# One block sum moved to VectorE, one gate/up set in plain form, and block sums over both depth halves at once, in a float32 decoder trunk

## The chip, the cores and the metric

The kernel runs on one core of a Trainium2 chip. The metric is the device time of one execution in microseconds (us). A row of times below comes from the hardware profile of one execution.

## What is computed

Four layers run one after the other on 256 tokens of width 1024, all in float32. Each layer is a SwiGLU feed-forward block (FFN), a token mixer with memory attention, and a second FFN, so there are eight FFNs. Only the FFN matters here:

```python
def swiglu_ffn(x, w_gate_up, w_down):
    gate, up = jnp.split(x @ w_gate_up, 2, axis=-1)
    return (jax.nn.silu(gate) * up) @ w_down
x = x + 0.5 * rms_norm(swiglu_ffn(rms_norm(x, g[0]), ffn_w_gate_up[i, 0], ffn_w_down[i, 0]), g[1])
```

The width of `gate` and of `up` is 2816.

## The kernel before, in words

**Precision.** A float32 operand is split in two (L311-313): ScalarE writes a high part `hi`, VectorE subtracts it to get the low part `lo`. A product takes three matmuls: hi·hi, hi·lo, lo·hi. Every weight tile of 128x1024 (512 KB) so costs one `hi` on ScalarE and one `lo` on VectorE before TensorE can use it. Ten such hi/lo pairs exist (the ring); plain weight tiles come through five `raw` buffers, loaded by SyncE in the order of use.

**Sets.** The 2816 columns of gate and up are worked in six sets of 4, 4, 2, 4, 4 and 4 column tiles of 128. Sets 0 and 4 are plain: 4 tiles of gate and 4 of up, each used for both halves of the tokens, 96 matmuls of 128x512 in all. Set 2, the narrow one, has 4 mixed tiles. Between the parts of the sets, `fill` puts in one or two tiles of the down projection (L696, 12 matmuls each).

**The 7-product form.** Sets 1, 3 and 5 (`SEVEN`) treat [two token halves x two depth halves] times [two depth halves x (gate, up)] as a 2x2 block product with 7 block products instead of 8: 84 matmuls of 128x512 (L624) rather than 96. The weight blocks, each a tile `quad` of 128x2x1024 (two quarters of the depth, index h), are x11 (gate, first depth half), x12 (up, first half), x21 (gate, second half) and x22 (up, second half, the far block). The products 0 to 6 use, in order, x11, x21, then x11+x12+x22, x12+x22, then x11+x12, the sum of all four, and x22. These are formed in place, one h at a time:

- x12 += x22, by an accumulating transfer that GpSimd issues (L271, called at L267) as soon as the second operand has been loaded. I call it the first sum.
- x11 += x12, by VectorE (L285), before the split for product 2: the second sum.
- x21 += x11, again by an accumulating transfer (L271, called from L286): the third sum.
- x11 -= x22, by VectorE (L288), before the split for product 4: the difference. It must follow the third sum, which reads x11.

**Joining the products.** `seven` (L636-671) gathers products 0 and 2 and then 3 and 5 in one PSUM bank, 1 in a second, 4 and 6 in a third. A `snap` (L632) on ScalarE copies a bank out before the next product adds to it: the copies after products 0, 2 and 3 are needed by products 2, 3 and 5. After product 4, VectorE computes the closing step of that bank (L655, `c22`: snap = c - U3); product 6 adds to the same bank, so its first matmul waits until the closing step has read it.

**Order.** Python emits the instructions in program order and a scheduler of the framework weaves them; each engine then runs its own list strictly in order. `slot` (called after each weight tile has been used) releases a hi/lo pair, issues one of the eight `quad` loads of the next 7-product set, if any is left, and lets up to two more splits go. The loads of a set are issued from slots of the set before it, on SyncE's queue between the `raw` loads, in the order x11, x21, x12, x22, two halves each; `quads_for` says how many of them a split needs.

Of the kernel before, what the change touches and what calls it, by code (L numbers as in the profile page):

```python
# [15 lines left out]
ALU = mybir.AluOpType  # L16
# [39 lines left out]
WIDTH = (4, 4, 2, 4, 4, 4)  # L56
SETS = len(WIDTH)
FIRST = tuple(sum(WIDTH[:s]) for s in range(SETS))
SEVEN = (1, 3, 5)
FILL = {1: (2, 2), 2: (2,), 3: (2, 0), 4: (1, 1), 5: (2, 2)}  # L60
QUADS = 8


def ffn_chunks(l, f):
    order = []
    nd = 0

    def fill(n):
        nonlocal nd, order
        order += [("D", l, f, nd + i) for i in range(n)]  # L70
        nd += n

    for s in range(SETS):
        if s in SEVEN:
            for ops, n in zip(((0, 1, 2), (3, 4, 5, 6)), FILL[s]):
                order += [("S", l, f, s, op, h) for op in ops for h in range(2)]
                fill(n)
            continue
        for c, n in zip(("e",) if WIDTH[s] == 2 else ("g", "u"), FILL.get(s, (0, 0))):
            order += [(c, l, f, s, i) for i in range(4)]  # L80
            fill(n)
    return order + [("D", l, f, j) for j in range(nd, NF)]
# [23 lines left out]
def plan():  # L106
    order = []
    for l in range(DEPTH):
        kind = l % 3
        order += ffn_chunks(l, 0)  # L110
        cols = [("C", l, c) for c in range(len(MIX_COLS[kind]))]
        for g, rng in enumerate(MIX_GROUPS[kind]):
            if g == 2:
                order += mem_units(l)
            order += [("R", l, g, k, n) for k, n in group_units(group_width(rng))]
            if g == 2:
                order += cols
        if len(MIX_GROUPS[kind]) == 2:
            order += mem_units(l) + cols
        order += [("O", l, j) for j in range(N_OUT[kind])]  # L120
        order += ffn_chunks(l, 1)
    return order
# [83 lines left out]
class Trunk:  # L206
# [53 lines left out]
    def load_quad(self):  # L260
        key = self.quad_loads.popleft()
        q, h = key[4:]
        if h == 0:
            pool, tag = ((self.main, "mgh"), (self.quad_pool, "q22"), (self.main, "mgl"), (self.main, "rows"))[q]
            self.quad[q] = pool.tile([P, 2, 1024], F32, tag=tag, name="quad")
        self.fetch(self.quad[q][:, h, :], key)
        if q == 3:  # L267
            self.gather(self.quad[1][:, h, :], self.quad[3][:, h, :])

    def gather(self, x, y):  # L270
        self.nc.gpsimd.dma_start(out=x, in_=y, accum_op=ALU.add)  # L271
# [1 line left out]
    def quads_for(self, key):  # L273
        if self.quad is None or self.quad_set != key[1:4]:
            return None
        return max(0, len(self.quad_loads) - (QUADS - ((2 * key[4] if key[4] < 2 else 6) + key[5] + 1)))

    def can_split(self):
        key = self.plan[self.split_n]
# [1 line left out]

    def operand(self, op, h):
        b11, b12, b21, b22 = (t if t is None else t[:, h, :] for t in self.quad)
        if op == 2:
            self.nc.vector.tensor_tensor(out=b11, in0=b11, in1=b12, op=ALU.add)  # L285
            self.gather(b21, b11)  # L286
        elif op == 4:
            self.nc.vector.tensor_tensor(out=b11, in0=b11, in1=b22, op=ALU.subtract)  # L288
        return (b11, b21, b11, b12, b11, b21, b22)[op]

    def split_next(self):
# [245 lines left out]
    def ffn(self, l, f, post_next, pre_next, last=False):  # L537
        nc, tc = self.nc, self.tc
        with tc.tile_pool(name=f"ffn{l}{f}", bufs=1, reuse_waits="tile") as fp:
# [8 lines left out]
            def tile_T():  # L548
                return fp.tile([P, 512], F32, tag="T", name="T", bufs=4)
# [21 lines left out]
            def first_set():  # L571
                T[0] = [tile_T(), tile_T()]
                held = [self.take("g", l, f, 0, i) for i in range(4)]
                for t in range(2):
                    g = self.rot()
                    for i in range(4):
                        pair(held[i], g, i, t)
                        self.slot(t)
                    silu(T[0][t], g)
                    u = self.rot()  # L580
                    if t == 0:
                        held.extend(self.take("u", l, f, 0, i) for i in range(4))
                    for i in range(4):
                        pair(held[4 + i], u, i, t)
                        self.slot(t)
                        if t == 0 and i == 2:
                            self.trans(1, keep=self.keep)
                    nc.vector.tensor_tensor(out=T[0][t], in0=T[0][t], in1=u, op=ALU.mult)
# [46 lines left out]
            def seven(s):  # L635
                tt = nc.vector.tensor_tensor  # L636
                v = {}
                a, b = self.rot(), self.rot()
                T0, T1 = T[s]
                keep = lambda n: lambda: v.__setitem__(n, snap(a))  # L640
                product(s, 0, a, True, keep("P1"))

                def c11():
                    tt(out=v["P1"], in0=v["P1"], in1=b, op=ALU.add)
                    silu(T0, v["P1"])

                product(s, 1, b, True, c11)
                turned(s - 1)
                product(s, 2, a, False, keep("U2"))
                fill(FILL[s][0])  # L650
                product(s, 3, a, False, keep("U3"))
                c = self.rot()

                def c22():
                    tt(out=v["U3"], in0=c, in1=v["U3"], op=ALU.subtract)  # L655

                product(s, 4, c, True, c22)

                def c21():
                    silu(T1, a)  # L660
                    tt(out=T1, in0=T1, in1=v["U3"], op=ALU.mult)

                product(s, 5, a, False, c21)

                def c12():
                    tt(out=v["U2"], in0=c, in1=v["U2"], op=ALU.subtract)
                    tt(out=T0, in0=T0, in1=v["U2"], op=ALU.mult)

                product(s, 6, c, False, c12)
                fill(FILL[s][1])  # L670

            self.new_quad(fp, l, f, 1)
            first_set()
            left = sums()
            gn = {"pre": None}
# [37 lines left out]
            for s in range(1, SETS):  # L713
                T[s] = [tile_T(), tile_T()]
                if s + 1 in SEVEN:
                    self.new_quad(fp, l, f, s + 1)
                if s in SEVEN:
                    seven(s)
                    if s == max(SEVEN):
                        self.bg.append(gains)  # L720
                    if s == max(SEVEN) and (l, f) == (0, 0):
                        self.bg.extend(self.setup2())
                    if s == min(SEVEN) and (l, f) == (0, 1):
                        self.bg.extend(self.rope_tables(fp))
# [623 lines left out]
```

## Time and profile before

| | |
|---|---|
| median of 3 runs | 1888.37 us (1885.9 to 1891.17) |
| the profiled execution, its own time | 1888.2 us |
| its span, first to last instruction | 1886.4 us |
| TensorE / VectorE / ScalarE / GpSimd busy | 1842.0 / 1537.1 / 1132.7 / 150.2 us |
| mean granted TensorE clock | 0.996 |
| weight loads of 512 KB through `raw` / `quad` | 440 / 192 |
| accumulating transfers of 512 KB | 96 |

How to read the rows: a row of a timeline gives the start, the length, the engine (PE TensorE, DVE VectorE, ACT ScalarE, POOL GpSimd, SP SyncE; "q" marks its DMA-issuing side), the line of the kernel, the operation, the tile written and the tiles read, the shape and a count; in square brackets stands how long the engine stood idle just before it, and what ended that. A row of the view of waits has who waited, for whom, the total in us, how many times, and the longest. A row of the windows has the stretch, its length, the busy time of PE, PE's weight loads, DVE, ACT and POOL with counts, the granted clock, the DMA share and GB/s.

### The profile page before, as it was taken

What the parts mean: (1) busy time and instruction counts of PE and PEld (TensorE: products, weight loads), DVE (VectorE), ACT (ScalarE), POOL (GpSimd) and SP (SyncE); (2) the same over time, 40 slices, a digit from 0 to 9 for tenths busy, and PEclk for the clock granted to TensorE, in tenths of its full rate; (3) what the DMA queues carried; (4) which work ended last, traced back from release to release, by engine and by line L of the source; (5) the groups of instructions that cost most, each with busy time, mean ns of one, the idle gap of its engine ahead of it and who ended that gap; (6) DMA issues with size and microseconds to landing.
All of it is one profiled execution on the core that took longest, in us unless ns stands there. A gap on an engine that the chain in (4) does not pass through costs nothing.

```text
span 1886.4 us, 25346 instructions
## 1 busy us (share of the span) xinstructions
PE 1842.0 (98%) x9310; PEld 1535.2 (81%) x9310; DVE 1537.1 (81%) x1868; ACT 1132.7 (60%) x1541; POOL 150.2 (8%) x211
## 2 busy tenths in 40 slices
PE   7999999999999999999999999999999999999998
PEld 5788887878788797778878889877788888987886
DVE  6888878987988768888789876879887988879884
ACT  5666656656665655656666666556665666656652
POOL 0000201000100100100010000010001000201000
PEclk9999999999999999999999999999999999999999
DMA  8886748776786662677668667358775786738862
GB/s 295 257 265 225 224 136 264 227 243 223 226 261 194 235 220 101 201 242 247 215 210 263 211 218 257 105 190 256 247 245 169 245 264 204 247 125 273 256 192 78
DMA packets 117692, 413.01 MB, mean 219 GB/s; under 512 B 13620, under 2 KB 18112, under 8 KB 117440
## 3 DMA queue, kind: packets, MB, share of 16 engines
q1 hardware_dynamic: 103568, 359.47, 54.2%
q0 software_dynamic: 14000, 51.92, 13.8%
q8 instruction: 73, 1.20, 0.3%
q14 instruction: 51, 0.42, 0.1%
HBM read 359.95 MB, written 1.06 MB: 191 GB/s over the span
## 4 chain that ended last, share of the span: by engine, by line
PE 41%; DVE 7%; DMA 3%; issue 2%; ACT 1%; POOL 1%; DVEq 0%; ACTq 0%; POOLq 0%
PE acc L696 12%; PE rot L624 9%; PE rot L337 5%; PE rot L339 5%; PE rot L338 5%; DVE lo L313 5%; PE acc L960 2%; DMA quad<-quad 2%; DMA quad<-in_w 1%; PE rot L565 1%; PE acc L880 1%; DVE quad L288 1%; PE rot L894 1%; PE rot L862 1%; ACT hi L312 0%
## 5 line engine op out<-in xcount | busy, mean ns | idle before, releaser
L313 DVE TENSOR_TENSOR lo<-raw,hi 128x1024 fp32r<-128x1024 f32 (+2 forms) x451 | 536.3, 1217 | 77.6 <-ACT hi L312 74.7
L312 ACT ACTIVATE hi<-raw 128x1024 fp32r<-128x1024 f32 (+2 forms) x451 | 463.2, 1051 | 198.3 <-DMA raw<-in_w 96.7
L312 ACT ACTIVATE hi<-quad 128x1024 fp32r<-128x1024 f32 x336 | 343.6, 1053 | 227.5 <-DVE quad L285 131.8
L313 DVE TENSOR_TENSOR lo<-quad,hi 128x1024 fp32r<-128x1024 f32 x336 | 397.5, 1219 | 20.7 <-ACT hi L312 19.9
L339 PE MATMUL rot<-hi,xtl 128*128 128x512 f32 (+3 forms) x816 | 312.8, 384 | 3.9 <-DVE xtl L313 3.9
L337 PE MATMUL rot<-hi,xth 128*128 128x512 f32 (+3 forms) x816 | 315.0, 386 | 0.4 <-ACT hi L312 0.4
L338 PE MATMUL rot<-lo,xth 128*128 128x512 f32 (+3 forms) x816 | 312.0, 382 | 0.3 <-DVE lo L313 0.3
L624 PE MATMUL rot<-hi,sums 128*128 128x512 f32 x768 | 255.1, 398 | 16.2 <-ACT snap L632 8.0
L696 PE MATMUL acc<-hi,hh 128*128 128x512 f32 x640 | 199.4, 391 | 0.0
L696 PE MATMUL acc<-lo,hh 128*128 128x512 f32 x640 | 198.9, 390 | 0.0
L696 PE MATMUL acc<-hi,hl 128*128 128x512 f32 x640 | 197.9, 390 | 0.0
L624 PEld LDWEIGHTS rot<-hi,sums 128*128 128x128 f32 x768 | 145.8, 190 | 52.9 <-ACT snap L632 12.3
L339 PEld LDWEIGHTS rot<-hi,xtl 128*128 128x128 f32 x816 | 153.7, 188 | 37.0 <-DVE xtl L313 8.3
L337 PEld LDWEIGHTS rot<-hi,xth 128*128 128x128 f32 x816 | 153.8, 189 | 29.2 <-ACT hi L312 1.0
L338 PEld LDWEIGHTS rot<-lo,xth 128*128 128x128 f32 x816 | 153.8, 188 | 29.2 <-DVE lo L313 0.5
L624 PE MATMUL rot<-lo,sums 128*128 128x512 f32 x384 | 151.2, 394 | 2.1 <-DVE lo L313 2.1
L271 POOL DMA_DIRECT2D quad<-quad x96 | 83.7, 897 | 837.6 <-DMA quad<-in_w 394.5
L696 PEld LDWEIGHTS acc<-hi,hl 128*128 128x128 f32 x640 | 119.6, 188 | 26.9 <-DVE hl L313 2.2
L696 PEld LDWEIGHTS acc<-lo,hh 128*128 128x128 f32 x640 | 119.9, 188 | 24.7
L696 PEld LDWEIGHTS acc<-hi,hh 128*128 128x128 f32 x640 | 119.7, 188 | 24.5
L624 PE MATMUL rot<-hi,xtl 128*128 128x512 f32 x288 | 112.1, 389 | 0.0
L624 PE MATMUL rot<-hi,xth 128*128 128x512 f32 x288 | 112.0, 389 | 0.0
(214 smaller groups left out, 2571.3 us busy)
## 6 DMA issues: line engine op xcount, KB each, us to landing
raw<-in_w SPq DMA_DIRECT2D x440, 512.0 KB, 4.8
quad<-in_w SPq DMA_DIRECT2D x192, 512.0 KB, 5.1
quad<-quad POOLq DMA_DIRECT2D x96, 512.0 KB, 4.7
gpre<-in_norm_g SPq DMA_DIRECT2D x8, 512.0 KB, 6.3
gpost<-in_norm_g SPq DMA_DIRECT2D x8, 512.0 KB, 3.4
memraw<-in_mem_t SPq DMA_DIRECT2D x32, 128.0 KB, 3.6
g<-in_norm_g SPq DMA_DIRECT2D x8, 512.0 KB, 6.7
raw<-in_w SPq DMA_DIRECT2D x8, 384.0 KB, 4.1
```

What stands on the lines that cost most here:

```text
L271: self.nc.gpsimd.dma_start(out=x, in_=y, accum_op=ALU.add)
L288: self.nc.vector.tensor_tensor(out=b11, in0=b11, in1=b22, op=ALU.subtract)
L312: self.nc.scalar.activation(out=hi, in_=src, func=AF.Copy)
L313: self.nc.vector.tensor_tensor(out=lo, in0=src, in1=hi.bitcast(F32), op=ALU.subtract)
L337: mm(out, a[0], b[0], start=start, stop=False)
L338: mm(out, a[0], b[1], start=False, stop=False)
L339: mm(out, a[1], b[0], start=False, stop=stop)
L565: nc.tensor.transpose(ps[:, k * P:(k + 1) * P], T[s][t][:, k * P:(k + 1) * P], self.ident)
L624: nc.tensor.matmul(ps, a[i], w[j][:, kk, :], start=fresh and h == kk == i == j == 0, stop=h == kk == i == 1, skip_group_check=True)
L696: mm(ys[t][:, n * 512:(n + 1) * 512], x, y[:, 0, n * 512:(n + 1) * 512], start=(j == 0 and x is a[0] and y is w[0]), stop=(j == NF - 1 and ...
L862: nc.tensor.transpose(ps[:, i * P:(i + 1) * P], blocks[b0 + i], self.ident)
L960: self.nc.tensor.matmul(o["y"][t][:, h * 512:(h + 1) * 512], x, y[:, 0, h * 512:(h + 1) * 512], start=(j == 0 and x is a[0] and y is w[0]) ...
```

## The change

Three things are changed. (a) In the first FFN of the first layer, set 1 is no longer in the 7-product form but plain, like sets 0 and 4. (b) In set 1 of the other seven FFNs the first sum, x12 += x22, is computed by VectorE at the time of the second sum; sets 3 and 5 keep the transfer for it. (c) All sums and differences of a 7-product set, and its transfers, work on both halves at once: one instruction of 128x2048 where two of 128x1024 stood, one transfer of 1 MB where two of 512 KB stood. A split for product 2 or later therefore needs all eight loads.

```diff
+def seven_sets(l, f):
+    return (1, 3, 5) if l or f else (3, 5)
...
-        if q == 3:
-            self.gather(self.quad[1][:, h, :], self.quad[3][:, h, :])
+        if q == 3 and h and key[3] > 1:
+            self.gather(self.quad[1], self.quad[3])
...
-        return max(0, len(self.quad_loads) - (QUADS - ((2 * key[4] if key[4] < 2 else 6) + key[5] + 1)))
+        return max(0, len(self.quad_loads) - (QUADS - (2 * key[4] + key[5] + 1 if key[4] < 2 else 8)))
...
-        if op == 2:
-            self.nc.vector.tensor_tensor(out=b11, in0=b11, in1=b12, op=ALU.add)
-            self.gather(b21, b11)
-        elif op == 4:
-            self.nc.vector.tensor_tensor(out=b11, in0=b11, in1=b22, op=ALU.subtract)
+        if h == 0 and op in (2, 4):
+            add = lambda x, y, f: self.nc.vector.tensor_tensor(out=x, in0=x, in1=y, op=f)
+            x11, x12, x21, x22 = self.quad
+            if op == 4:
+                add(x11, x22, ALU.subtract)
+            else:
+                if self.quad_set[2] == 1:
+                    add(x12, x22, ALU.add)
+                add(x11, x12, ALU.add)
+                self.gather(x21, x11)
         return (b11, b21, b11, b12, b11, b21, b22)[op]
...
+            SEVEN = seven_sets(l, f)
+            if 1 in SEVEN:
+                self.new_quad(fp, l, f, 1)
```

The lines of the changed kernel are numbered 8 to 10 higher (L313 is L321, L655 is L663, L624 is L632); its sums and differences all stand in L288, its transfers in L274.

VectorE in set 1 of the second layer's first FFN, before the change, from the split of product 1's second half on (L546 is a silu, `sums` and `xf` are sums of the activations, L588 the product with up in set 0):

```order
L313 TENSOR_TENSOR lo<-quad,hi 128x1024
L313 TENSOR_TENSOR sums<-xf,sums 128x512
L285 TENSOR_TENSOR quad<-quad 128x1024
L546 SCALAR_TENSOR_TENSOR T<-T,rot 128x512
L285 TENSOR_TENSOR quad<-quad 128x1024
L313 TENSOR_TENSOR lo<-quad,hi 128x1024
L313 TENSOR_TENSOR sums<-xf,sums 128x512
L313 TENSOR_TENSOR lo<-quad,hi 128x1024
L313 TENSOR_TENSOR lo<-raw,hi 128x1024 x2
L313 TENSOR_TENSOR lo<-quad,hi 128x1024
```

The same place after the change:

```order
L321 TENSOR_TENSOR lo<-quad,hi 128x1024
L288 TENSOR_TENSOR quad<-quad 128x2048
L554 SCALAR_TENSOR_TENSOR T<-T,rot 128x512
L288 TENSOR_TENSOR quad<-quad 128x2048
L321 TENSOR_TENSOR sums<-xf,sums 128x512
L596 TENSOR_TENSOR T<-T,rot 128x512
L321 TENSOR_TENSOR lo<-quad,hi 128x1024 x2
L321 TENSOR_TENSOR lo<-raw,hi 128x1024 x2
L321 TENSOR_TENSOR lo<-quad,hi 128x1024
L321 TENSOR_TENSOR sums<-xf,sums 128x512
```

The first sum has come in as a row of its own, the second is one wide row, and both splits of product 2 stand behind both.

VectorE in set 3 of the same FFN before the change, from the second sum's second half on (L546 and L733 finish the narrow set 2, L644 joins products 0 and 1, `el` is a split of the hidden activations of set 2):

```order
L285 TENSOR_TENSOR quad<-quad 128x1024
L733 TENSOR_TENSOR T<-T,rot 128x256
L546 SCALAR_TENSOR_TENSOR T<-T,rot 128x256
L733 TENSOR_TENSOR T<-T,rot 128x256
L313 TENSOR_TENSOR lo<-quad,hi 128x1024
L313 TENSOR_TENSOR lo<-raw,hi 128x1024 x2
L313 TENSOR_TENSOR lo<-quad,hi 128x1024 x3
L288 TENSOR_TENSOR quad<-quad 128x1024
L644 TENSOR_TENSOR snap<-snap,rot 128x512
L313 TENSOR_TENSOR lo<-quad,hi 128x1024
L546 SCALAR_TENSOR_TENSOR T<-T,snap 128x512
L313 TENSOR_TENSOR el<-rot,eh 128x2x128 x2
```

Then follow four splits of `quad`, five of `raw` and the closing step L655. After the change, from the second sum to the closing step L663:

```order
L288 TENSOR_TENSOR quad<-quad 128x2048
L321 TENSOR_TENSOR lo<-quad,hi 128x1024 x2
L321 TENSOR_TENSOR lo<-raw,hi 128x1024 x2
L321 TENSOR_TENSOR lo<-quad,hi 128x1024
L652 TENSOR_TENSOR snap<-snap,rot 128x512
L321 TENSOR_TENSOR lo<-quad,hi 128x1024
L554 SCALAR_TENSOR_TENSOR T<-T,snap 128x512
L321 TENSOR_TENSOR el<-rot,eh 128x2x128 x2
L288 TENSOR_TENSOR quad<-quad 128x2048
L321 TENSOR_TENSOR lo<-quad,hi 128x1024 x6
L321 TENSOR_TENSOR lo<-raw,hi 128x1024 x4
L663 TENSOR_TENSOR snap<-rot,snap 128x512
```

Everything of the first half (its second sum, the split of product 2, its difference) has moved behind the transfer for both halves; the steps of set 2 now all stand ahead of the wide sum, and the six splits of products 4 to 6 all stand behind the wide difference.

More of the change, by code (lines that the diff above doesn't have):

```diff
@@ L58 @@
 FIRST = tuple(sum(WIDTH[:s]) for s in range(SETS))
-SEVEN = (1, 3, 5)
 FILL = {1: (2, 2), 2: (2,), 3: (2, 0), 4: (1, 1), 5: (2, 2)}
 QUADS = 8
+def seven_sets(l, f):
+    return (1, 3, 5) if l or f else (3, 5)
 def ffn_chunks(l, f):
@@ L73, in ffn_chunks @@
     for s in range(SETS):
-        if s in SEVEN:
+        if s in seven_sets(l, f):
             for ops, n in zip(((0, 1, 2), (3, 4, 5, 6)), FILL[s]):
@@ L670, in seven @@
                 fill(FILL[s][1])
-            self.new_quad(fp, l, f, 1)
+            SEVEN = seven_sets(l, f)
+            if 1 in SEVEN:
+                self.new_quad(fp, l, f, 1)
             first_set()
```

## Prediction

> **What bounds the kernel now.** I read the page first, then TensorE's waits, then the stretches in which TensorE loses time.
>
> ```profile
> PE 1842.0 (98%) x9310; PEld 1535.2 (81%) x9310; DVE 1537.1 (81%) x1868; ACT 1132.7 (60%) x1541; POOL 150.2 (8%) x211
> PE rot L624 <- ACT snap L632: 8.0, 10, 1.6
> PE rot L624 <- DVE snap L655: 4.7, 5, 2.6
> PE rot L624 <- ACT hi L312: 3.4, 1, 3.4
> PE rot L624 <- DVE lo L313: 2.1, 1, 2.1
> ```
>
> TensorE is busy nearly throughout, so a step elsewhere counts only where TensorE then waits. In the 7-product sets it waits for three things: ScalarE's copies, VectorE's closing step L655, and, in the third and fourth rows, once each for a weight split that isn't ready. Those two lie together, in set 1 of the first FFN:
>
> ```profile
> 39.19 1.97 POOL L271 DMA_DIRECT2D quad<-quad  x2 [23.14 <-DMA quad<-in_w]
> 41.80 1.03 PE L565 MATMUL rot<-ident,T 128*128 128x128 f32 x8
> 46.23 0.51 PE L624 MATMUL rot<-hi,sums 128*128 128x512 f32 x1 [3.40 <-ACT hi L312]
> 48.80 0.79 PE L624 MATMUL rot<-lo,sums 128*128 128x512 f32 x1 [2.06 <-DVE lo L313]
> 42.83:54.51 11.68, 6.22 (x15) 4.64 (x15) 10.64 (x11) 7.11 (x9) 1.74 (x2) 0.72 0.84 187
> ```
>
> The first sum starts only at 39.19, when the far block has landed, and TensorE is at product 2 by 42.83. It runs 15 matmuls in the next 11.68 us, partly at a reduced clock (0.72 in the mean).
>
> What a matmul of 128x512 costs on the path is the distance of two starts; these two rows are where product 5 ends and product 6 begins in set 3 of layer two's first FFN:
>
> ```profile
> 567.72 0.39 PE L624 MATMUL rot<-hi,xtl 128*128 128x512 f32 x1
> 567.95 0.45 PE L624 MATMUL rot<-hi,sums 128*128 128x512 f32 x1
> ```
>
> That is 0.227 us. All sums are made against the profiled execution's own time, 1888.2 us, which is the median (1888.37) within 0.2.
>
> **(a) The first FFN's set 1 in plain form.** It removes the loss: 11.68 less 15 x 0.227 = 3.4, so 8.3 us. It adds 96 - 84 = 12 matmuls, 2.7 us. Its eight tiles come as `raw`, whose splits need no sum, and there are fewer of them (8 against 14), so VectorE and ScalarE have room. One `lo` (1.2 us) moves ahead of the activations' split on VectorE near 24 us, which TensorE waits for; I take half, 0.6. Sum: -5.0, between -4.4 and -5.6.
>
> **(b) Set 1 of the other seven FFNs.** What the added instruction costs follows from sizes that are in the trace:
>
> ```profile
> L607 DVE TENSOR_TENSOR xf<-xf 128x512 f32<-128x512 f32 x32 | 22.1, 690 | 1.0
> L285 DVE TENSOR_TENSOR quad<-quad 128x1024 f32<-128x1024 f32 x48 | 58.7, 1224 | 44.4 <-DMA quad<-quad 44.1
> ```
>
> 512 columns more cost 0.53 us, so 128x2048 takes 1.22 + 2 x 0.53 = 2.3 us, 2.2 where it overlaps its neighbours. Two narrow instructions or one wide one cost the same, so only the first sum is new: 7 x 2.2 = 15.4 us of VectorE. What does it replace? The idle time in which VectorE waited for the transfer. I quote the first and the last of ten such rows in these seven sets; the ten sum to 9.1 us:
>
> ```profile
> 311.96 1.23 DVE L285 TENSOR_TENSOR quad<-quad 128x1024 f32<-128x1024 f32 x1 [0.77 <-DMA quad<-quad]
> 1721.61 1.23 DVE L285 TENSOR_TENSOR quad<-quad 128x1024 f32<-128x1024 f32 x1 [0.63 <-DMA quad<-quad]
> ```
>
> Does VectorE's lateness reach TensorE? In set 1 of layer two's first FFN:
>
> ```profile
> 505.29 2.35 DVE L288 TENSOR_TENSOR quad<-quad 128x1024 f32<-128x1024 f32 x2
> 521.31 0.68 DVE L655 TENSOR_TENSOR snap<-rot,snap 128x512 f32<-128x512 f32 x1
> 522.36 0.39 PE L624 MATMUL rot<-hi,sums 128*128 128x512 f32 x1
> ```
>
> No row of VectorE's from the difference to the closing step has idle time before it; the step ends at 521.99, and product 6 starts at 522.36: 0.33 us of cover beyond the hand-over. So the balance is 15.4 - 9.1 - 7 x 0.33 = +4.0 us. It could be as low as -4 if TensorE gets back ScalarE's copies (below), and +6 if none of the cover counts. Queued behind the new sum are the silu and all splits; the transfer of the third sum is no longer behind another one on GpSimd's queue and lands well ahead of the difference.
>
> **(c) Set 3 of the seven FFNs.** Here the transfer stays, and must now wait for the last load. I work the case with no wait at present, in layer two's first FFN:
>
> ```profile
> 529.34 0.53 SPq L242 DMA_DIRECT2D quad<-in_w  x1
> 538.24 0.88 POOL L271 DMA_DIRECT2D quad<-quad  x1 [1.63 <-DMA quad<-in_w]
> 540.45 0.38 ACT L545 ACTIVATE T<-rot 128x256 f32<-128x256 f32 x1 [0.98 <-PE rot L339]
> 542.90 1.23 DVE L285 TENSOR_TENSOR quad<-quad 128x1024 f32<-128x1024 f32 x1 [0.87 <-DMA quad<-quad]
> 544.22 1.06 ACT L312 ACTIVATE hi<-quad 128x1024 fp32r<-128x1024 f32 x1 [3.38 <-DVE quad L285]
> 545.31 1.23 DVE L313 TENSOR_TENSOR lo<-quad,hi 128x1024 fp32r<-128x1024 f32 x1
> 554.53 1.23 DVE L313 TENSOR_TENSOR lo<-quad,hi 128x1024 fp32r<-128x1024 f32 x1 [0.59 <-ACT hi L312]
> 567.16 0.68 DVE L655 TENSOR_TENSOR snap<-rot,snap 128x512 f32<-128x512 f32 x1
> 545.70 0.39 PE L624 MATMUL rot<-hi,xth 128*128 128x512 f32 x1
> ```
>
> The last load lands just before 538.24, because the first half's transfer and eight loads share the DMA engines with it. With that transfer gone it should take what a lone load takes, 3.27, plus one tile's turn behind the load ahead of it, 512 KB at 417 GB/s = 1.26, less the 0.4 between their issues: 4.1, landing at 533.5.
>
> ```profile
> 1339.19 3.27 DMA quad<-in_w
> 29.33:36.36 7.03, 7.03 (x33) 5.82 (x32) 6.56 (x9) 5.53 (x7) 0.00 (x0) 1.00 1.02 417
> 1448.32 0.88 POOL L271 DMA_DIRECT2D quad<-quad  x1 [6.22 <-DVE xf L607]
> 1449.54 5.83 DMA quad<-quad
> ```
>
> The 1 MB transfer is bounded by a pair of 512 KB that run into one another: from 1448.32 to 1455.37, 7.05 us; with other loads about, the longest such pair takes 8.5. I take 7.05: it lands at 540.9 with GpSimd's 0.3. But VectorE's wide sum stands behind set 2's last steps, which the tanh at 540.45 releases: 0.38 + 0.42 + 0.42, so 541.6. Both meet there. The sum ends at 543.9, `hi` (1.06 and 0.1 of hand-over) at 545.05: that is 0.25 earlier than now. From there to the closing step VectorE has the same 16 splits, but the difference is twice as wide (+1.1) and two bubbles open: the split of product 4 waits for a `hi` behind the wide difference (1.16 where 0.59 stood), and that of product 3 for one behind ScalarE's copy of product 0 (0.7). So the 21.85 us of now become 24.2, and the closing step starts at 569.3, not 567.16. TensorE's product 6 starts 0.11 after its present end, so it waits: +2.0 us.
>
> The seven sets 3 would lose 14 us by that. But some of them wait already, and those waits are not paid twice: L655's 4.7 us, all in sets 3; 1.4 for the clock after its longest; and two copies:
>
> ```profile
> 843.98 0.50 PE L624 MATMUL rot<-hi,sums 128*128 128x512 f32 x1 [1.27 <-ACT snap L632]
> 1330.41 0.50 PE L624 MATMUL rot<-hi,sums 128*128 128x512 f32 x1 [1.02 <-ACT snap L632]
> ```
>
> In all 8.4, so +5.6. One set has its last load issued late, 13.8 us ahead of product 0 instead of 16.4; there the sum starts 1.4 later:
>
> ```profile
> 822.93 0.42 SPq L242 DMA_DIRECT2D quad<-in_w  x1
> 836.66 0.39 PE L624 MATMUL rot<-hi,xth 128*128 128x512 f32 x1
> ```
>
> Sum for sets 3: +7.0. Ends: 0, if VectorE's order leaves the closing step where it is; +19, if each transfer lands 1.7 later.
>
> **(d) Set 5, and sets 3 and 5 of the first FFN.** VectorE's steps after the wide sum wait for set 4's end anyway, and from there to the closing step I count as much work as TensorE has products: no loss, +0.8 for the eight together, at most +4.
>
> **The rivals.**
> - *VectorE's lateness does not reach product 6; the copies come earlier (faster).* In set 1 both halves of product 2 are split 1.2 us earlier than the second half now, and ScalarE's copy of product 2 stands ahead of the split behind the difference, so the 8.0 us of L632 would go. It decides if VectorE reaches the closing step of set 1 no later than now: the idle taken out must be 2.2 us a set. For it: in one set it is 2.7. Against it: in four it is under 0.8. With sets 3 unchanged: 1888.2 - 5.0 - 8.0 = 1875.
> - *The waits of sets 3 also slow the clock (slower).*
>
> ```profile
> 386.54 0.80 PE L624 MATMUL rot<-hi,sums 128*128 128x512 f32 x1 [2.62 <-DVE snap L655]
> 386.00:390.30 4.30, 3.76 (x11) 3.00 (x12) 3.82 (x5) 2.60 (x3) 0.00 (x0) 0.61 0.94 341
> 1280.05 0.50 PE L624 MATMUL rot<-hi,sums 128*128 128x512 f32 x1 [1.56 <-ACT snap L632]
> 1280.39 0.39 PE L624 MATMUL rot<-lo,sums 128*128 128x512 f32 x1
> ```
>
> After 2.62 us without work the granted clock is 0.61 over the next matmuls, 1.4 us lost; after 1.56 the next follows at once. My waits of 2.0 lie between. Seven times 1.4 more gives 1905. [...]
> - *The 1 MB transfers are slow, 8.5 us or more:* 1.7 more in each of seven sets 3, about 1907.
> - *The change does nothing on balance:* (a) is eaten up by late `raw` loads, since the DMA engines are full at that time (1.02 in the window at 29.33); with (b) to (d) half as large, 1888 to 1892.
>
> **How the numbers follow.** -5.0 + 4.0 + 7.0 + 0.8 = +6.8, so 1895.0 us. About 0.3%, 5.7 us, is what a measurement can tell from no change: 1882.5 to 1893.9. Chances: the forecast 0.52, its own range 1889 to 1901, of which some 0.24 falls below 1893.9; faster 0.20; clock 0.14; slow transfers 0.10; nothing 0.04. So faster 0.20, same 0.28, slower 0.52. The range reaches to the rivals' near parts: 1879 to 1909.
>
> **What would show it.** In the profile after: no gap between 42 and 55 us and set 2's first product about 5 us earlier; the waits for L632 under 8; the waits for the closing step, L663, near 15 to 20 us in some 14 rows of about 1 to 2 us, no longer 4.7 in 5; GpSimd's transfers 7 us from issue to landing. I am wrong if the waits for L663 stay under 8 us, or if VectorE in set 3 reaches the closing step within 22 us of the first split of product 2.

## The result, and the profile after

| | before | after |
|---|---|---|
| median of 5 runs each, us | 1887.29 (1882.92 to 1891.17) | 1902.47 (1899.6 to 1905.83) |
| ratio, 95% interval | | 1.0080 (1.0058 to 1.0102) |
| the profiled execution / its span, us | 1888.2 / 1886.4 | 1899.6 / 1897.8 |
| mean granted TensorE clock | 0.996 | 0.998 |

The change makes the kernel slower by 0.8%, some 15 us; forecast were 1895.0, slower, and 1879 to 1909. The time lies in that range, which reaches to the rivals, and 1.5 us above the forecast's own, 1889 to 1901; and it does not lie there for the reasons given. In the changed kernel the copies stand at L640, the closing step at L663, the splits at L320 (`hi`) and L321 (`lo`), the 7-product matmuls at L632, the down projection at L706; all of VectorE's block sums stand at L288. Its page and its view of TensorE's waits:

```profile
PE 1848.2 (97%) x9322; PEld 1533.5 (81%) x9322; DVE 1533.3 (81%) x1816; ACT 1116.2 (59%) x1532; POOL 99.2 (5%) x154
...
quad<-quad POOLq DMA_DIRECT2D x39, 1024.0 KB, 7.3
```

```profile
PE rot L411 <- DVE rows L397: 14.1, 9, 8.2
PE rot L632 <- ACT snap L640: 9.3, 15, 0.9
PE rot L632 <- DVE snap L663: 5.2, 6, 1.0
PE rot L347 <- DVE xtl L321: 4.9, 6, 1.5
PE rot L345 <- ACT hi L320: 3.8, 7, 0.9
...
PE acc L706 <- ACT hh L320: 0.8, 1, 0.8
```

The closing step makes TensorE wait 5.2 us in 6 rows, about as before (4.7 in 5); I had forecast 15 to 20 in 14. All 6 lie in sets 5 and none in sets 3, where all 5 lay before. The wait for `hi` at L345 has grown from 0.4 us in one row to 3.8 in 7. The totals hide where these lie, so I went through all of TensorE's rows: the distance of two starts, less what the second needs by its size at the full clock (0.227 us for 512 columns), is time lost, a lowered clock included. Taken against the usual distance of each pair of shapes instead, the two sums below are 68.7 and 77.0: some 42 us are alike in both runs, and only differences tell something. Summed by place:

| lost, us | set 1 | set 3 | set 5 | elsewhere | sum |
|---|---|---|---|---|---|
| before | 23.6 | 11.8 | 2.7 | 72.5 | 110.6 |
| after | 7.2 | 17.9 | 12.3 | 82.0 | 119.4 |

Of the 23.6, 9.2 are the first FFN's set 1, which is no longer there, and 14.4 the other seven. The sum grows by 8.8; the 12 added matmuls take 2.7: together 11.5, and the spans differ by 11.4.

**Set 1.** The first FFN's gap is closed, at the full clock, and product 0 of its set 3 starts at 88.76 in place of 93.23:

```profile
42.83:54.51 11.68, 11.68 (x57) 9.78 (x56) 8.94 (x10) 6.43 (x10) 0.00 (x0) 1.00 0.93 312
```

In set 1 of layer two's first FFN, where the prediction had the closing step late, the timeline now shows:

```profile
521.43 0.68 DVE L663 TENSOR_TENSOR snap<-rot,snap 128x512 f32<-128x512 f32 x1
```

```profile
495.61 0.39 PE L632 MATMUL rot<-hi,xth 128*128 128x512 f32 x1
...
519.64 0.62 PE L706 MATMUL acc<-lo,hh 128*128 128x512 f32 x2
...
522.36 0.62 PE L706 MATMUL acc<-hi,hl 128*128 128x512 f32 x2
522.81 0.39 PE L632 MATMUL rot<-hi,sums 128*128 128x512 f32 x1
```

The step ends at 522.11, and product 6 starts 0.70 us later without waiting. VectorE did not get there earlier. Product 0 starts at 495.61, before the change at 496.79:

```profile
496.79 0.39 PE L624 MATMUL rot<-hi,xth 128*128 128x512 f32 x1
```

Counted from there, the step ends after 26.50 us in place of 25.20; but product 6 starts after 27.20 in place of 25.57. Between products 0 and 6 TensorE now does 42 matmuls of the down projection where 33 stood (14 of them behind product 5, where 9 stood): the scheduler has put nine more, some 2.0 us of work, ahead of product 6. Over the seven sets the step ends 0.7 us later in the mean, and product 6 starts 1.0 later. What TensorE no longer loses there is above all the waits for ScalarE's copies: 5.7 us in 8 rows of these sets before, 1.3 in 3 after.

**Set 5.** The same FFN; first before (product 0 at 598.8), then after (product 0 at 599.1). VectorE's block sums, GpSimd's transfer, and what TensorE waits for at product 6:

```profile
590.21 1.23 DVE L285 TENSOR_TENSOR quad<-quad 128x1024 f32<-128x1024 f32 x1 [3.03 <-DMA quad<-quad]
...
592.68 1.23 DVE L288 TENSOR_TENSOR quad<-quad 128x1024 f32<-128x1024 f32 x1
...
596.47 1.22 DVE L288 TENSOR_TENSOR quad<-quad 128x1024 f32<-128x1024 f32 x1 [1.43 <-issue]
```

```profile
595.65 2.29 DVE L288 TENSOR_TENSOR quad<-quad 128x2048 f32<-128x2048 f32 x1 [8.64 <-DMA quad<-quad]
606.16 2.29 DVE L288 TENSOR_TENSOR quad<-quad 128x2048 f32<-128x2048 f32 x1
598.48 0.86 POOL L274 DMA_DIRECT2D quad<-quad  x1 [8.87 <-DVE quad L288]
622.20 0.68 DVE L663 TENSOR_TENSOR snap<-rot,snap 128x512 f32<-128x512 f32 x1
622.94 0.50 PE L632 MATMUL rot<-hi,sums 128*128 128x512 f32 x1 [0.98 <-DVE snap L663]
```

Before, VectorE formed both differences ahead of product 0. Now it stands idle for 8.64 us, sums at 595.65, and the difference follows the third sum's transfer (issued at 598.48) at 606.16, 7 us behind product 0. The work that was done in idle time is now queued ahead of the closing step.

**Set 3**, layer two's first FFN, product 0 at 544.1:

```profile
542.86 2.29 DVE L288 TENSOR_TENSOR quad<-quad 128x2048 f32<-128x2048 f32 x1 [2.70 <-DMA quad<-quad]
...
546.33 2.36 DVE L321 TENSOR_TENSOR lo<-quad,hi 128x1024 fp32r<-128x1024 f32 x2 [1.19 <-ACT hi L320]
...
569.85 0.68 DVE L663 TENSOR_TENSOR snap<-rot,snap 128x512 f32<-128x512 f32 x1
```

```profile
557.39 5.80 ACT L320 ACTIVATE hi<-quad 128x1024 fp32r<-128x1024 f32 x6 [3.54 <-DVE quad L288]
...
564.99 0.58 ACT L640 ACTIVATE snap<-rot 128x512 f32<-128x512 f32 x1
```

```profile
564.20 0.50 PE L345 MATMUL rot<-hi,xth 128*128 128x512 f32 x1 [0.40 <-ACT hi L320]
565.62 0.50 PE L632 MATMUL rot<-hi,xth 128*128 128x512 f32 x1 [0.92 <-ACT snap L640]
```

ScalarE stands idle 3.54 us for the wide difference and then has six `hi` in a row; the copy that product 5 needs stands behind those and two more. TensorE waits there, ahead of the closing step. Behind product 5 the scheduler has put ten matmuls of set 4, where product 6 followed at once before:

```profile
568.47 0.39 PE L346 MATMUL rot<-lo,xth 128*128 128x512 f32 x1
...
570.51 0.40 PE L346 MATMUL rot<-lo,xth 128*128 128x512 f32 x1
570.74 0.39 PE L632 MATMUL rot<-hi,sums 128*128 128x512 f32 x1
```

So the closing step, which ends at 570.53, holds up nothing.

Over the whole kernel the sums show the same in one grouped row (before, then after): the idle time ahead of VectorE's sums that a transfer ended was 44.1 us at L285 and 3.7 at L288, and is now 90.0.

```profile
L285 DVE TENSOR_TENSOR quad<-quad 128x1024 f32<-128x1024 f32 x48 | 58.7, 1224 | 44.4 <-DMA quad<-quad 44.1
L288 DVE TENSOR_TENSOR quad<-quad 128x1024 f32<-128x1024 f32 x48 | 57.9, 1222 | 21.9 <-issue 17.3 <-DMA quad<-quad 3.7 <-DVE lo L313 0.3
```

```profile
L288 DVE TENSOR_TENSOR quad<-quad 128x2048 f32<-128x2048 f32 x53 | 121.2, 2286 | 95.1 <-DMA quad<-quad 90.0 <-issue 4.8 <-DVE lo L321 0.2
```

### The profile page after: what moved, and what is told of

It is laid out like the page before. It is cut to its first block, busy times and chain, and to the rows that moved or that the text cites. A ratio compares the mean times of both kernels' runs of the same rounds, so it can differ in the third digit from the quotient of the medians.

```text
span 1897.8 us, 25146 instructions
## 1 busy us (share of the span) xinstructions
PE 1848.2 (97%) x9322; PEld 1533.5 (81%) x9322; DVE 1533.3 (81%) x1816; ACT 1116.2 (59%) x1532; POOL 99.2 (5%) x154
## 4 chain that ended last, share of the span: by engine, by line
PE 51%; DVE 19%; DMA 15%; issue 6%; ACT 6%; POOL 1%; SPq 1%; ACTq 0%; POOLq 0%; DVEq 0%
PE acc L706 12%; DVE lo L321 11%; PE rot L632 10%; PE rot L347 7%; PE rot L346 7%; PE rot L345 7%; DMA quad<-in_w 6%; DMA quad<-quad 4%; ACT hi L320 4%; DMA raw<-in_w 4%; PE acc L970 3%; DVE quad L288 3%; DMA memraw<-in_mem_t 2%; PE rot L573 1%; PE rot L872 1%
## 5 line engine op out<-in xcount | busy, mean ns | idle before, releaser
L321 DVE TENSOR_TENSOR lo<-raw,hi 128x1024 fp32r<-128x1024 f32 (+2 forms) x459 | 548.7, 1225 | 55.8 <-ACT hi L320 54.1
L320 ACT ACTIVATE hi<-raw 128x1024 fp32r<-128x1024 f32 (+2 forms) x459 | 469.3, 1049 | 179.8 <-DMA raw<-in_w 90.3
L320 ACT ACTIVATE hi<-quad 128x1024 fp32r<-128x1024 f32 x322 | 322.7, 1049 | 266.2 <-DVE quad L288 217.6
L321 DVE TENSOR_TENSOR lo<-quad,hi 128x1024 fp32r<-128x1024 f32 x322 | 380.9, 1219 | 32.2 <-ACT hi L320 32.1
L345 PE MATMUL rot<-hi,xth 128*128 128x512 f32 (+3 forms) x848 | 327.8, 387 | 4.2 <-ACT hi L320 3.8
L347 PE MATMUL rot<-hi,xtl 128*128 128x512 f32 (+3 forms) x848 | 324.8, 383 | 4.9 <-DVE xtl L321 4.9
L346 PE MATMUL rot<-lo,xth 128*128 128x512 f32 (+3 forms) x848 | 324.4, 383 | 0.6 <-DVE lo L321 0.6
L632 PE MATMUL rot<-hi,sums 128*128 128x512 f32 x736 | 243.7, 396 | 8.8 <-DVE snap L663 5.2
L706 PE MATMUL acc<-hi,hh 128*128 128x512 f32 x640 | 197.2, 391 | 0.8 <-ACT hh L320 0.8
L288 DVE TENSOR_TENSOR quad<-quad 128x2048 f32<-128x2048 f32 x53 | 121.2, 2286 | 95.1 <-DMA quad<-quad 90.0
L706 PE MATMUL acc<-lo,hh 128*128 128x512 f32 x640 | 197.8, 390 | 0.0
L706 PE MATMUL acc<-hi,hl 128*128 128x512 f32 x640 | 197.2, 389 | 0.4 <-DVE hl L321 0.4
L345 PEld LDWEIGHTS rot<-hi,xth 128*128 128x128 f32 x848 | 159.5, 188 | 37.3 <-ACT hi L320 7.1
L632 PEld LDWEIGHTS rot<-hi,sums 128*128 128x128 f32 x736 | 138.0, 188 | 46.2 <-ACT snap L640 9.6
L632 PE MATMUL rot<-lo,sums 128*128 128x512 f32 x368 | 143.6, 390 | 0.0
L706 PEld LDWEIGHTS acc<-hi,hl 128*128 128x128 f32 x640 | 120.1, 188 | 25.8 <-DVE hl L321 0.8
L706 PEld LDWEIGHTS acc<-hi,hh 128*128 128x128 f32 x640 | 118.8, 188 | 26.2 <-ACT hh L320 2.6
L706 PEld LDWEIGHTS acc<-lo,hh 128*128 128x128 f32 x640 | 119.6, 188 | 24.5
L632 PE MATMUL rot<-hi,xth 128*128 128x512 f32 x276 | 108.7, 394 | 6.0 <-ACT snap L640 6.0
L632 PE MATMUL rot<-hi,xtl 128*128 128x512 f32 x276 | 108.2, 392 | 0.0
```

What stands on the lines that cost most here:

```text
L288: add = lambda x, y, f: self.nc.vector.tensor_tensor(out=x, in0=x, in1=y, op=f)
L320: self.nc.scalar.activation(out=hi, in_=src, func=AF.Copy)
L321: self.nc.vector.tensor_tensor(out=lo, in0=src, in1=hi.bitcast(F32), op=ALU.subtract)
L345: mm(out, a[0], b[0], start=start, stop=False)
L346: mm(out, a[0], b[1], start=False, stop=False)
L347: mm(out, a[1], b[0], start=False, stop=stop)
```

## The experiments

Three batches of four, each beside the kernel before on the same chip (1886.88, 1886.48 and 1885.83 us). Ratios, with the 95% interval, are to that; they are estimated from the single runs and can differ a little from the quotient of the medians.

| run | us | ratio | set 1 | set 3 | set 5 | elsewhere |
|---|---|---|---|---|---|---|
| e1, first FFN plain alone | 1885.27 | 0.9997 (0.9987 to 1.0007) | 14.2 | 10.0 | 2.7 | 82.1 |
| e2, VectorE's first sum in set 1 alone | 1886.17 | 0.9996 (0.9984 to 1.0009) | 20.3 | 8.1 | 2.7 | 77.7 |
| e3, both halves at once alone | 1956.89 | 1.0370 (1.0356 to 1.0383) | 48.4 | 19.4 | 15.1 | 96.8 |
| e4, after, sets 3 and 5 by halves | 1879.60 | 0.9964 (0.9952 to 0.9976) | 7.1 | 11.2 | 3.1 | 77.9 |
| e5, first transfer by halves | 1906.74 | 1.0106 (1.0093 to 1.0120) | 6.9 | 18.7 | 14.6 | 86.3 |
| e6, third transfer, difference by halves | 1901.64 | 1.0086 (1.0069 to 1.0103) | 7.0 | 16.8 | 10.6 | 85.4 |
| e7, both transfers by halves | 1907.76 | 1.0109 (1.0095 to 1.0123) | 7.1 | 19.6 | 14.0 | 83.8 |
| e8, set 5 by halves | 1891.28 | 1.0022 (1.0013 to 1.0031) | 7.0 | 16.0 | 5.4 | 82.7 |
| e9, first sum by halves | 1902.85 | 1.0087 (1.0069 to 1.0105) | 7.0 | 11.3 | 24.8 | 79.0 |
| e10, e4 with after's rule on loads | 1880.39 | 0.9973 (0.9963 to 0.9984) | 7.0 | 11.7 | 2.7 | 77.3 |
| e11, e4 with VectorE's first sum in set 5 | 1878.49 | 0.9961 (0.9949 to 0.9973) | 7.2 | 10.8 | 2.7 | 77.5 |
| e12, a and b, all by halves | 1882.90 | 0.9980 (0.9972 to 0.9989) | 14.4 | 4.9 | 2.7 | 79.4 |

The last four columns are TensorE's lost time as above, of each run's profiled execution.

**e1, e2, e3: each part alone, on the kernel before; e4: all but part c in sets 3 and 5.**

> The kernel before with one part of the change alone: set 1 of the first FFN in plain form. All theories: the gap of 8.3 us goes and 12 matmuls come, so 4.5 us faster than before (as the profile after has it at the start of the first FFN's set 3), between 1882 and 1884 beside a before of 1887.3. If it brings less than 3 us, the first FFN's gain is given back later, and the plain form is not what the change earns.

> The kernel before with one part alone: in set 1 of all eight FFNs VectorE makes the first sum, each half by itself; nothing else is wide, sets 3 and 5 are as before, and the first FFN keeps its 7-product form. Theory A (the large transfers cost the time, and VectorE's added sum is free because TensorE's other work fills in): 0.5 to 1.5 us faster in each set 1, so 1878 to 1884. Theory B (VectorE is the bound, as in the prediction's part b): 1 to 4 us slower than before, 1888 to 1892.

> The kernel before with one part alone: both depth halves at once in all 7-product sets, the first sum by transfer in all of them, the first FFN's set 1 included. Theory A (two transfers of 1 MB in series make the difference late): what sets 3 and 5 lose after the change, 6 and 10 to 16 us, and 1 us or more in each set 1 too, so 15 to 25 us slower than before, 1902 to 1912, with the waits for ScalarE's copies and for the closing step in all three sets. Theory B (VectorE's work is the bound): the wide instructions cost VectorE no more than the narrow ones and the added sum is left out, so at most 8 us slower, 1895 or less. Theory C (the losses after the change come from a shifted order of other work): anywhere, but with the loss outside the 7-product sets.

> The changed kernel with sets 3 and 5 put back to halves (transfers, sums and differences as before); set 1 keeps VectorE's wide sums, and the first FFN's set 1 stays plain. Theory A: the gains of set 1 stay, 4.5 and 7.0 us, and what sets 3 and 5 lost comes back, so 1874 to 1879, faster than both. Theory B: part b costs 4 us and part a gains 4.5 to 5, so 1885 to 1889. Theory C: set 1's gain was order as well, 1880 to 1890, with the losses at the mixers and the ends of the FFNs still there.

```diff
# e1, against before
-SEVEN = (1, 3, 5)
+    return (1, 3, 5) if l or f else (3, 5)
# e2, against before
-        if q == 3:
+        if q == 3 and key[3] > 1:
...
         if op == 2:
+            if self.quad_set[2] == 1:
+                add(b12, b22, ALU.add)
# e3, against after
-    return (1, 3, 5) if l or f else (3, 5)
+    return (1, 3, 5)
...
-        if q == 3 and h and key[3] > 1:
+        if q == 3 and h:
...
-                if self.quad_set[2] == 1:
-                    add(x12, x22, ALU.add)
# e4, against after
-        if q == 3 and h and key[3] > 1:
-            self.gather(self.quad[1], self.quad[3])
+        if q == 3 and key[3] > 1:
+            self.gather(self.quad[1][:, h, :], self.quad[3][:, h, :])
...
-        return max(0, len(self.quad_loads) - (QUADS - (2 * key[4] + key[5] + 1 if key[4] < 2 else 8)))
+        return max(0, len(self.quad_loads) - (QUADS - (2 * key[4] + key[5] + 1 if key[4] < 2 else 8 if key[3] == 1 else 6 + key[5] + 1)))
...
+        if self.quad_set[2] > 1:
...
+            if op == 2:
+                add(b11, b12, ALU.add)
+                self.gather(b21, b11)
+            elif op == 4:
+                add(b11, b22, ALU.subtract)
```

e1 misses: 1.6 us faster by the medians, 0.6 by the ratio, not 4.5. In its profile the plain form's 8.3 us do come, but are lost again 30 us later. VectorE and TensorE in the first FFN, e1's timelines, and the window behind the wait:

```profile
83.91 1.23 DVE L287 TENSOR_TENSOR quad<-quad 128x1024 f32<-128x1024 f32 x1 [1.40 <-DMA quad<-quad]
85.05 1.28 DVE L317 TENSOR_TENSOR hl<-rot,hh 128x512 fp32r<-128x512 f32 x2
```

```profile
85.79 1.22 PE L702 MATMUL acc<-hi,hl 128*128 128x512 f32 x2 [3.06 <-DVE hl L317]
```

```profile
85.79:90.00 4.21, 4.21 (x10) 3.34 (x11) 4.13 (x7) 0.35 (x1) 0.00 (x0) 0.50 0.27 79
```

With plain tiles in set 1, set 3's blocks arrive early, and VectorE takes up their second difference, which waits 1.40 us for its transfer. The activation's low part `hl` stands behind it on VectorE, and the down projection waits 3.06 us for that, then runs at a granted clock of 0.50 over 4.21 us. After the change the same place waits for the high part `hh` instead, 0.8 us (the last row of the waits above). The wait for `hl` is there in every run with part a and set 3 wholly by halves, but e1's profile shows the worst of it, and it is of the slowest of e1's eleven runs (1889.32). In e4, e10, e11 and e12 the wait is 2.38, 2.81, 1.82 and 2.32 us, and product 0 of set 3 starts at 89.70, 90.11, 90.91 and 89.76, against 93.23 before and 93.34 in e1. So by halves part a keeps 2.3 to 3.5 us in those profiles, where the profile after has 4.5; why e1's median gains so little is not shown.

e2 is where neither theory put it: no gain, no loss that can be told. e3 is far beyond theories A and B, and C, which gave no figure, wanted the loss outside the sets: it is 70 us slower, with 25 us more lost in set 1, 20 in sets 3 and 5 and 24 "elsewhere". Set 1 of layer one's second FFN, GpSimd, VectorE and TensorE:

```profile
321.22 0.90 POOL L274 DMA_DIRECT2D quad<-quad  x1 [12.28 <-DVE lo L319]
328.11 2.29 DVE L288 TENSOR_TENSOR quad<-quad 128x2048 f32<-128x2048 f32 x1 [2.10 <-DMA quad<-quad]
```

```profile
336.76 0.76 PE L630 MATMUL rot<-hi,sums 128*128 128x512 f32 x1 [5.04 <-ACT snap L638]
```

With the first sum by one transfer for both halves, issued at 321.22, VectorE can sum only at 328.11, and the copy that TensorE needs comes behind ScalarE's splits of that sum. After the change, with VectorE's first sum there, sets 1 lose 7.2 us. So part c is bearable in set 1 only together with part b; the two can't be added up one by one.

e4 shows that set 1's gain is real and that part c costs its time in sets 3 and 5: 7 us faster than before, some 22 faster than after, and 0.6 above theory A's range. It beats both kernels.

**e5 to e8: which piece of part c.**

> The changed kernel with one thing put back: in sets 3 and 5 the first sum's transfer goes by halves again, each half issued with its own load; VectorE's sums, the third sum's transfer and the differences stay at once. The changed kernel runs 1902.5, the one with sets 3 and 5 wholly by halves 1879.6: 22.9 us to share out. Theory A1 (the first transfer costs it: it starts with the last load and takes 7 us): most of it comes back, 1883 to 1888. Theory A2 (the third sum's transfer costs it: the difference waits for its landing): little, 1896 to 1902, since the sum still waits for the second half. Theory B (the wide sum and difference on VectorE tie the first half to the second): little, 1896 to 1902, too.

> The changed kernel with one thing put back: in sets 3 and 5 the third sum's transfer and the difference go by halves; the first sum's transfer and VectorE's sum stay at once. Theory A1: little comes back, 1896 to 1902. Theory A2: most of it, 1882 to 1888, and the waits for the closing step in set 5 go. Theory B: the difference's part of it, about a half, 1890 to 1896.

> The changed kernel with both transfers of sets 3 and 5 by halves (two of 512 KB in place of each of 1 MB), and VectorE's sum and difference still wide. Theories A1 and A2 (it is the size of the transfers): 1879 to 1885. Theory B (it is the wide instruction, which waits for both halves, that costs, whatever the transfers' size): 1895 or more.

> The changed kernel with set 5 alone put back to halves, set 3 still at once. TensorE's lost time within set 5 is 12.3 us after the change and 3.1 with halves, so 9.2 us come back in set 5 by every theory. Theory S (the 5.4 us that the ends of the FFNs and the mixers lose more belong to set 5 too, since its lateness reaches what stands behind it on VectorE and ScalarE): 1887 to 1889. Theory C (they come from an order shifted elsewhere): 1892 to 1895. By the prediction's parts c and d set 3 costs 7.0 and set 5 0.8: then only about 1 us would come back, 1901.

```diff
# against after: e5 (and in e7)
-        if q == 3 and h and key[3] > 1:
-            self.gather(self.quad[1], self.quad[3])
+        if q == 3 and key[3] > 1:
+            self.gather(self.quad[1][:, h, :], self.quad[3][:, h, :])
# e7 besides, in sets 3 and 5
-                self.gather(x21, x11)
+                    for j in range(2):
+                        self.gather(x21[:, j, :], x11[:, j, :])
# e6, in sets 3 and 5
-                self.gather(x21, x11)
+                self.gather(b21, b11)
...
-                add(x11, x22, ALU.subtract)
+                add(b11, b22, ALU.subtract)
# e8: the lines of e4, for set 5 alone
+        if self.quad_set[2] == 5:
```

Theories A1 and A2 fall. With all transfers of 512 KB (e7) nothing comes back; e5 and e7 are no faster than the changed kernel. It is not the size of the transfers; what is left is VectorE's wide instructions, which tie the halves. Theory B, which says that, has e7 right, but e5 came in 5 us above its range, and e6, for which it had half of the loss coming back, brings nothing back. e8 gives 11 us back by set 5 alone, more than the 7 that the table shows in set 5 itself; the time lies between theories S and C. The profiled spans differ by only 8.4, since the changed kernel's profile is of its fastest run.

**e9 to e12: the sum or the difference, the landing or the order, and two versions.**

> In sets 3 and 5 the first sum goes by halves again, its transfer and VectorE's addition; the third sum's transfer and the difference stay at once, and set 1 is as in the changed kernel. Theory L (what costs is that the sum of the first half waits for the landing of the second: VectorE starts its work for the set some 6 us later, having stood idle, and the backlog reaches the closing step): most of the 22.9 us come back, 1879 to 1886. Theory W (any wide instruction that ties the halves costs, the difference too): about a half, 1888 to 1895. Theory A2 (the third sum at once): 1895 or more.

> The kernel with sets 3 and 5 wholly by halves, and of the change there only its rule on the program's order: the first half's sum stands in the program behind the issue of all eight loads, not of seven. Theory L (the landing that the sum waits for): 1879.6 as without the rule, at most 1884. Theory G (the later place in the program, behind more of the set before, is what costs): 1892 to 1902.

> The kernel with sets 3 and 5 by halves, and set 5's first sum by VectorE as well, by halves, without its transfer: 16 more instructions of 1.23 us in the eight sets, 19.7 us, at a place where VectorE stands idle for 5.6 us before the sum. TensorE loses only 3.1 us within sets 5 there, so theory L sees no more than 2 us to be had, 1877 to 1880. Theory B (VectorE is the bound): 4 to 12 us slower, 1884 to 1892.

> The plain form in the first FFN and VectorE's first sum in set 1, but everything by halves: the two earlier runs that each had one of these, taken together (1885.3 and 1886.2 beside 1886.9). If the two add, 1884 to 1885, and set 1's gain of the changed kernel comes from the wide form there. If the first sum by VectorE is what gains and the earlier run lost it again in the first FFN, 1879 to 1881, as with set 1 at once.

```diff
# e9, against e4
+        halves = self.quad_set[2] > 1
+        if op == 4:
+            if h == 0:
                 add(x11, x22, ALU.subtract)
...
+        elif op == 2:
+            if halves:
+                add(b11, b12, ALU.add)
...
+            if h == (1 if halves else 0):
                 self.gather(x21, x11)
# e10, against e4
-        return max(0, len(self.quad_loads) - (QUADS - (2 * key[4] + key[5] + 1 if key[4] < 2 else 8 if key[3] == 1 else 6 + key[5] + 1)))
+        return max(0, len(self.quad_loads) - (QUADS - (2 * key[4] + key[5] + 1 if key[4] < 2 else 8)))
# e11, against e4
-        if q == 3 and key[3] > 1:
+        if q == 3 and key[3] == 3:
...
+                if self.quad_set[2] == 5:
+                    add(b12, b22, ALU.add)
# e12: e1 and e2 together
```

e10 rules out theory G: the later place in the program costs nothing that can be told (1880.39 beside e4's 1879.60). e9 was forecast at 1879 to 1886 by theory L, at 1888 to 1895 by theory W and at 1895 or more by theory A2, and came in at 1902.85, where A2 alone had it. The table says why L missed: set 3 is as good as by halves (11.3), which is theory L's part, but set 5 lost more than in any other run. GpSimd, VectorE and TensorE in set 5 of layer two's first FFN, e9's timelines:

```profile
592.75 0.86 POOL L274 DMA_DIRECT2D quad<-quad  x1 [6.99 <-DVE quad L287]
600.65 2.29 DVE L287 TENSOR_TENSOR quad<-quad 128x2048 f32<-128x2048 f32 x1 [4.87 <-issue]
602.86 1.22 DVE L325 TENSOR_TENSOR lo<-raw,hi 128x1024 fp32r<-128x1024 f32 x1
604.00 1.28 DVE L756 TENSOR_TENSOR T<-T,rot 128x512 f32<-128x512 f32 x2
```

```profile
604.73 1.26 PE L577 MATMUL rot<-ident,T 128*128 128x128 f32 x8 [1.61 <-DVE T L756]
```

VectorE reaches the wide difference early and stands idle for 4.87 us ahead of it; it starts at 600.65, 7.9 us after the third sum of both halves was issued (592.75). The row names no releaser; that the landing of this transfer ends the wait is my reading. Set 4's last step, `T`, is queued behind, and TensorE waits for it, with closing steps late besides. In e6 the wide sum does the harm; VectorE in the same set:

```profile
595.09 2.29 DVE L287 TENSOR_TENSOR quad<-quad 128x2048 f32<-128x2048 f32 x1 [10.13 <-DMA quad<-quad]
...
606.01 2.36 DVE L287 TENSOR_TENSOR quad<-quad 128x1024 f32<-128x1024 f32 x2
```

The sum starts at 595.09, and the differences, narrow again, follow only at 606.01. So in set 5 either wide instruction puts the first half's difference behind the second half's transfers, and in the whole kernel undoing one while the other stays gives nothing back; set 3 alone recovers with the sum (e9). In e9 the third sum's transfer stays at once like the difference. No run parts these two: a pair of 512 KB took 7.05 us in the trace of before, so in e7, where that transfer goes by halves, a wide difference would by this estimate wait nearly as long.

e11 shows the same by its opposite: 16 instructions more on VectorE in set 5, where it is idle, cost nothing (1878.49 beside e4's 1879.60, the intervals overlap). e12 lies between: in set 1 it loses 14.4 us, as before, and it is the wide form there that has 7.1; set 3 gives most of that back, 4.9 in place of 11.2. So of e4's gain the wide form in set 1 would have about 3 us, but the two intervals overlap a little, so that is not certain.

## Why the prediction was right in sum and wrong in its terms

| term | forecast | measured in the profiles |
|---|---|---|
| a, first FFN's set 1 | -5.0 | -4.5 |
| b, set 1 of seven FFNs | +4.0 | 7.2 - 14.4 = -7.2 |
| c, sets 3 | +7.0 | 17.9 - 11.8 = +6.1 |
| d, sets 5 | +0.8, at most +4 | 12.3 - 2.7 = +9.6 |
| elsewhere | 0 | the rest: +7.4 |

The measured column sums to +11.4, the difference of the spans; the medians differ by 15.2. That the sum fell so near is luck: part b is 11.2 us too high, part d 8.8 and the rest 7.4 too low, and they cancel.

- **a** held in size. What the step lacked is that set 3's loads come earlier after it, and with halves that costs 1 to 2 us of the gain (e4, e10 to e12), in e1's profile all of it. The prediction counted only what set 1 itself saves.
- **b** failed in sign. VectorE's own balance was about right: by the sum the closing step should come (15.4 - 9.1) / 7 = 0.9 us later a set, and counted from product 0 it comes 0.7 later. The step that failed took TensorE's order as fixed: "0.33 us of cover beyond the hand-over". The order moved, nine more matmuls stand ahead of product 6, and the closing step has 0.5 to 0.7 us to spare. The sum also left out the waits for the copies, which fell from 5.7 to 1.3 us in sets 1. That is of the first rival's kind, though not by its condition, since VectorE is later in five of the seven sets; and in sets 3 and 5 the same waits rose from 2.3 to 8.1 us, so 9.3 in all, where that rival had them gone and the forecast had them under 8.
- **c** held in size, by luck, and nearly in VectorE's rows: the sum was forecast at 541.6 and starts at 542.86, the closing step at 569.3 and starts at 569.85, and from the first split of product 2 to it are 23.5 us against 24.2; a transfer takes 7.3 us in the median, against 7.05. But the transfer is issued only at 535.98, where the last load was forecast to land at 533.5; and product 0 comes 1.6 us earlier than before, so that counted from it the step is 4.3 us later, not 2.1. TensorE does not wait for it all the same: ten matmuls of set 4 now stand ahead of product 6, again an order that the sum took as fixed, and it has already waited for ScalarE's `hi` and copy at product 5. I had worked only VectorE's queue; the wide difference also holds ScalarE's.
- **d** is the step that failed most. "VectorE's steps after the wide sum wait for set 4's end anyway" held for the steps of set 4, not for the set's own differences, which the trace of before had ahead of product 0 (592.68 and 596.47). The prediction counted the work from the wide sum to the closing step and not what had been done before it in idle time. The view that would have told it is the timeline of set 5 before, which I did not quote.
- **elsewhere**: 3.3 us of the rest lie between the first FFN's set 5 and the second FFN, in several short waits, most of them for VectorE. With set 5 by halves (e4, e8) that loss is gone, so it hangs on set 5. Another 2.9 us, between the seventh FFN's set 5 and the eighth FFN, are lost in e4 and e8 as well. What causes these, and the remaining 1.2, stays open.
- Of the rivals, slow transfers can be ruled out as the cause (e7; 7.3 us in the median, not 8.5). The clock in sets 3 fell in one of the seven alone, where that rival had it in all: 0.66 over 1044 to 1048 us, behind waits of 0.58 and 0.93 us, some 1.6 us lost. In the changed kernel no wait inside the sets is longer than 1.0 us. Late `raw` loads, the last rival, did not eat up part a, which gave 4.5 us. By the prediction's own test (the waits for L663 under 8 us) its mechanism for part c was wrong in place.

## What to carry to other kernels

Two halves of a chain of load, sum, transfer, difference are a pipeline: one instruction over both halves makes the first half wait for the second half's last transfer, and the idle time ahead of it does not come back. Here that cost some 22 us, and undoing one link alone (e6, e9) brought none of it back. So count what an engine does early, in its idle time, before merging it with something late, and look at every engine that is queued behind the merged instruction. And the order in which a scheduler places other work is no constant: cover measured in the trace of before moved by nine or ten matmuls. Where all inputs are already there (set 1, with the sum on VectorE) the wide form costs nothing and may gain a little; parts of a change that lean on each other are worth measuring in pairs, not only alone.

## What the runs showed of the hardware

**The clock behind a wait is not set by the wait's length alone.** At one place in the first FFN, TensorE waits for `hl` in the runs with part a and set 3 wholly by halves, for different lengths. After 3.06 us (e1) the clock is 0.50. After 2.81 us it is 1.00, after 1.82 us 0.62; e10 and then e11, the wait and the window behind it:

```profile
85.45 0.73 PE L713 MATMUL acc<-hi,hl 128*128 128x512 f32 x2 [2.81 <-DVE hl L328]
...
85.20:89.20 4.00, 3.75 (x16) 3.12 (x17) 4.00 (x8) 1.06 (x1) 0.00 (x0) 1.00 0.17 42
```

```profile
84.62 0.73 PE L715 MATMUL acc<-hi,hl 128*128 128x512 f32 x2 [1.82 <-DVE hl L330]
...
84.62:88.62 4.00, 4.00 (x11) 3.21 (x12) 4.00 (x7) 0.90 (x1) 0.00 (x0) 0.62 0.24 66
```

So the prediction's reading, a threshold between 1.56 and 2.62 us, was too simple. In sets 3 of the changed kernel the next 4 us have a clock of 0.64 behind a wait of 0.93 us at 1042.16, and of 1.00 behind one of 0.93 us at 1801.01. What decides it is not shown.

**A wide instruction on VectorE saves little by itself.** One of 128x2048 takes 2.286 us in the mean; two of 128x1024 that follow one another take 2.35 together (505.29 in the prediction's rows): 0.06 us a pair. Two narrow ones of 1.224 us, the mean, would take 0.16 more if each ran by itself; back to back, 0.10 of that overlaps.
